# Hybrid SSD / RG-LRU block: output projections as seven half-block products, FFN pairs with running sums in PSUM

## The chip, the cores and the metric

The kernel runs on one core of one Trainium2 chip. The metric is the device time of one execution in microseconds, as the median of three runs. A profile is one more execution, recorded by the hardware profiler; its times are measured from the first instruction of its span. The engines are TensorE (PE in the profile, with its weight loads as PEld), VectorE (DVE), ScalarE (ACT), GpSimd (POOL) and SyncE (SP), which issues all the data transfers of this kernel.

## The reference, cut to what matters

One layer, 1024 tokens, width 1024, float32. The change concerns the two output projections, the merge of their results, and the gate/up products of the FFN:

```python
hn = rmsnorm(h, norm1_w)
proj = hn @ w_in                                   # gates, z, xBC, dt, lru_x, lru_y
y_ssm = mamba2_mixer(...) @ w_out_ssm              # 2048 -> 1024
y_lru = rglru_mixer(...) @ w_out_lru               # 1280 -> 1024
h = h + (g_ssm * y_ssm + g_lru * y_lru) @ w_out    # 1024 -> 1024
hn = rmsnorm(h, norm2_w)
gate, up = split(hn @ w_ffn_in, 2)                 # 1024 -> 2 x 2816
h = h + (silu(gate) * up) @ w_ffn_out              # 2816 -> 1024
return rmsnorm(h, norm_f_w)
```

## The kernel before

Activations lie transposed: features on the 128 partitions, tokens along the row, in two token halves of 512 (`hcol`). A float32 product is made of three matmuls with operands rounded to fp32r: every operand is split into a high part (a cast on ScalarE, L99) and the rest (a subtraction on VectorE, L100), and `mm3` (L168 to 177) or `product` (L947 to 954) issues hi·hi, lo·hi and hi·lo for each 128-row block of the contraction, 128x128 weights against 128x512 activations, into one PSUM bank. All instructions are laid in order by a scheduler at compile time: on each engine the earliest instruction of the program that is ready by its own reckoning comes next, and a tile takes whichever buffer of its pool is free. The chip then runs each engine's list strictly in order.

The stages that matter here, in order of time:

1. **Input projection, with the SSD and then the LRU mixer beside it.** The last part loops over ten LRU blocks `j`: two projections of 48 matmuls and `lru_gates(j)` (L780 to 815). Mixer outputs go to DRAM as 128x1024 tiles, `yn_d[0..15]` (SSD) and `yl_d[0..9]` (LRU). Before the last two gate projections the kernel already loads and splits the first half of `yn_d[0..7]` (`y0`, L831).
2. **SSD output projection** (L868 to 884): the 2048 rows in two halves `q`; for each `q`, each of 8 output column tiles `d` and both token halves a product of 8 blocks, 24 matmuls. At `q` = 0 the bank is copied into `res[d]` by ScalarE (L879), at `q` = 1 it is added by VectorE (L881) and the sum is scaled by the gate (L883).
3. **LRU output projection** (L887 to 900): for each `d` and half one product of 10 blocks, 30 matmuls; VectorE scales it by its gate (L895) and adds it to `res` (L896), and the merged `mg` is split into operands.
4. **w_o stage** (from L973): 16 products of 24 matmuls, the residual added from `xT`, squares summed on POOL (L864), and in its second half the differences `t1` to `t4` for the FFN made on VectorE by `t_parts` (L956 to 967).
5. **FFN pairs**: the gate and up tiles of one hidden block `n` are taken as a 2x2 block product with seven half-block products instead of eight (12 matmuls each, `product`); `first_pair` (L1017) and then 21 times `pair` (L1051). POOL makes the weight sums (`pair_sums`, L924 to 933). Partial results stand in several banks (`px`, `pv`, `py`, `pz`) and are put together on VectorE in `c0` and `c1`.
6. **FFN output** (L1090 to 1207): rows 0 to 2047 in two parts of eight blocks; each part is a seven-product scheme over four pairs of column tiles (`d` and `d + 4`). A part has 14 slots (seven products `N2, N5, N3, N1, N6, N7, N4`, each for two groups `g` of two column pairs), and each slot has 24 matmuls. Loads, weight sums (`w_sum`, POOL, L1158 and L1161), operand splits (`x_part`, `w_part`) and products are hung on slots: `w_part` of a product one slot ahead, its `x_part` two. The operands `act_d` and their differences `t_d` come from DRAM; the differences are made by `t_store` on VectorE while the pairs run. After each product VectorE adds the bank to `res` (L1206).
7. The last 6 hidden blocks by plain products, the final norm and the stores.

Pools that the steps touch: `wpool` holds `raw`, `whi`, `wlo` with two buffers each; `ar` 22 units, `ar0` 8, `br` 6 and `wq` 5 units of 128x1024; `pb` the 8 PSUM banks; `sp1` 5 and `tp` 10 tiles of 128x512.

Of the kernel before, what the change touches and what calls it, by code (L numbers as in the profile page):

```python
# [8 lines left out]
F32 = mybir.dt.float32  # L9
# [6 lines left out]
P = 128  # L16
# [44 lines left out]
NTMP = 10  # L61
# [7 lines left out]
def hybrid_block(ctx, tc, xT, w_in, w_dt, w_os, w_ol, w_o, w_fi, w_fo, w_fl, lru_w, params, heads, out):  # L69
# [66 lines left out]
    wseq += [(w_os[d, q], 8) for q in range(2) for d in range(KD)]  # L136
    wseq += [(w_ol[d, :, 5 * q : 5 * q + 5], 5) for d in range(KD) for q in range(2)]
# [6 lines left out]
    wstop = [wseq_out]  # L144
# [137 lines left out]
    res_d = [dram.tile([P, T], F32, name=f"res_d{i}") for i in range(KD)]  # L282
    t_d = [dram.tile([P, T], F32, name=f"t_d{i}") for i in range(8 * NPART)]
    act_d = [dram.tile([P, T], F32, name=f"act_d{i}") for i in range(NFF)]

# [3 lines left out]
    with ExitStack() as st1:  # L289
# [474 lines left out]
        with tc.tile_pool(name="lru", bufs=1, reuse_waits="tile", side="right") as lp, tc.tile_pool(  # L764
# [51 lines left out]

            for j in range(NLRU):
                project_now(lx_done(j))
                project_now(lg_done(j))
                lru_gates(j)  # L820

# [30 lines left out]
    def load_acts(pool, srcs, h):  # L852
        return [act_pair(pool, load_half(s[:, hcol[h]])) for s in srcs]

    def mm_act(ps, w, xs):
        mm3(ps, lambda k: (w[0][:, k, :], w[1][:, k, :]), xs)

    def sumsq(acc, src, first):
        if first:
            S.activation(acc, src, AF.Square)  # L860
        else:
            sq = temp("sq2")
            S.activation(sq, src, AF.Square)  # L863
            G.tensor_tensor(acc, acc, sq, op=ALU.add)  # L864


    res = [unit(br if d < 6 else ar, F32, "res") for d in range(KD)]
    for q in range(2):  # L868
        yn = [
            y0 if q == 0 and h == 0 else load_acts(ar0 if h == 0 else ar, yn_d[q * 8 : q * 8 + 8], h) for h in range(2)  # L870
        ]
        for d in range(KD):
            w = next_w()
            for h in range(2):
                ps = bank()
                mm_act(ps, w, yn[h])
                r = res[d][:, h, :]
                if q == 0:
                    S.copy(r, ps)  # L879
                else:  # L880
                    V.tensor_tensor(r, r, ps, op=ALU.add)  # L881
                    gt = load_half(gate_d[d][:, hcol[h]], "gt")
                    V.scalar_tensor_tensor(r, gt, 1.0, r, op0=ALU.add, op1=ALU.mult)  # L883


    yl = [load_acts(ar, yl_d, h) for h in range(2)]
    mg = [[None] * KD for _ in range(2)]  # L887
    for d in range(KD):
        w = next_w(), next_w()
        for h in range(2):  # L890
            ps = bank()
            mm3(ps, lambda k: (w[k // 5][0][:, k % 5, :], w[k // 5][1][:, k % 5, :]), yl[h])
            r = res[d][:, h, :]
            gt = load_half(gate_d[8 + d][:, hcol[h]], "gt")
            V.scalar_tensor_tensor(gt, gt, 1.0, ps, op0=ALU.add, op1=ALU.mult)  # L895
            V.tensor_tensor(r, r, gt, op=ALU.add)  # L896
        mg[0][d] = act_pair(ar0, res[d][:, 0, :])
    for d in range(KD):
        mg[1][d] = act_pair(ar, res[d][:, 1, :])
# [9 lines left out]
    row = lambda t_: t_.rearrange("p a b -> p (a b)")  # L909
# [15 lines left out]
    def pair_sums(n):  # L925
# [5 lines left out]
        G.tensor_tensor(u_[:, 0:4, :], u_[:, 0:4, :], g_[:, 0:4, :], op=ALU.add)  # L931
        G.tensor_tensor(g_[:, 0:4, :], g_[:, 0:4, :], blk(s1), op=ALU.add)
        G.tensor_tensor(g_[:, 4:8, :], g_[:, 4:8, :], g_[:, 0:4, :], op=ALU.add)
# [13 lines left out]
    def product(ps, w, xs, first, last):  # L947
        n = len(xs)
        for k in range(n):
            wh, wl = w[0][:, k, :], w[1][:, k, :]  # L950
            xh, xl = xs[k]
            PE.matmul(ps, wh, xh, start=first and k == 0, stop=False, skip_group_check=True)  # L952
            PE.matmul(ps, wl, xh, start=False, stop=False, skip_group_check=True)  # L953
            PE.matmul(ps, wh, xl, start=False, stop=last and k == n - 1, skip_group_check=True)  # L954

    def t_parts(x, k, u1, u2, pool):  # L956


# [10 lines left out]

# [4 lines left out]
    for h in range(2):  # L974
        for i, d in enumerate(wo_order[h]):
# [14 lines left out]
            if h == 0:  # L990
                bn[d] = unit(br if d not in (0, 4) else ar, F32, "bn")
# [58 lines left out]
    def pair(n, nxt, pump):  # L1050
# [36 lines left out]
        finish_pair(n, c0, c1)  # L1087

# [311 lines left out]
```

## Time and profile before

| | us |
|---|---|
| median of three runs | 2101.86 (2101.03 to 2103.66) |
| the profiled execution | 2103.04 |
| its span, first to last instruction | 2101.2 |
| PE busy | 2056.3 (98%) |
| DVE busy | 1300.4 (62%) |
| ACT busy | 868.8 (41%) |
| POOL busy | 448.2 (21%) |

Matmuls overlap, so that PE's busy time says little about single matmuls: one is recorded with some 390 ns, while in an undisturbed stretch one starts every 227 ns. What a stage costs is therefore read from the length of its window and its count of matmuls; waits of PE and its granted clock show where it fell behind.

### The profile page before, as it was taken

How to read it: one execution, taken by the hardware profiler on the slowest of the kernel's cores; microseconds unless marked ns; L12 is line 12 of the kernel's file. 1: busy time of each engine (PE TensorE's matmuls, PEld its weight loads, DVE VectorE, ACT ScalarE, POOL GpSimd, SP SyncE). 2: the span in 40 equal slices, each digit the busy share in tenths (PEclk: the TensorE clock that was granted, in tenths of full speed). 3: DMA queues.
4: the chain of work that ended last, by engine and by line, in shares of the span. 5: the costliest groups of instructions: out<-in, count | busy, mean ns of one | idle time of the engine just before them, and what ended most of it. 6: DMA issues, size and time to landing. Idle time of an engine off the chain costs nothing.

```text
span 2101.2 us, 24820 instructions
## 1 busy us (share of the span) xinstructions
PE 2056.3 (98%) x9650; PEld 1669.8 (79%) x9650; DVE 1300.4 (62%) x1582; ACT 868.8 (41%) x1227; POOL 448.2 (21%) x390
## 2 busy tenths in 40 slices
PE   8999999999999999999999999998999999989998
PEld 6677887887887888888878888876887888877888
DVE  8655567568667546655513543578577577588745
ACT  5334445445445436666523221453222222234334
POOL 5103333234333410000000000123322332342200
PEclk8999999999999999999999999999999999999999
DMA  3222223323223242221334532452244254286122
GB/s 141 89 60 87 89 76 118 100 67 120 93 76 115 89 145 81 69 77 65 105 115 146 153 120 63 149 177 77 79 173 154 75 180 161 86 290 209 61 59 87
DMA packets 106500, 235.22 MB, mean 112 GB/s; under 512 B 11920, under 2 KB 30352, under 8 KB 106384
## 3 DMA queue, kind: packets, MB, share of 16 engines
q1 hardware_dynamic: 106384, 233.66, 33.6%
q8 instruction: 75, 1.23, 0.2%
q14 instruction: 41, 0.34, 0.1%
HBM read 183.02 MB, written 50.59 MB: 111 GB/s over the span
## 4 chain that ended last, share of the span: by engine, by line
PE 83%; DVE 7%; DMA 3%; ACT 3%; issue 2%; POOL 1%; SPq 1%; DVEq 0%; ACTq 0%
PE pj L177 11%; PE pj L175 11%; PE pj L176 11%; PE pbk L952 8%; PE pbk L953 8%; PE pbk L954 8%; PE pbk L175 7%; PE pbk L177 7%; PE pbk L176 7%; PE yb L662 1%; DVE wlo L100 1%; PE yb L650 1%; DVE xs L495 1%; PE tr L628 1%; DMA ld<-yn_d 1%
## 5 line engine op out<-in xcount | busy, mean ns | idle before, releaser
L175 PE MATMUL pj<-hnh,whi 128*128 128x512 f32 x1152 | 461.1, 400 | 0.0
L177 PE MATMUL pj<-hnl,whi 128*128 128x512 f32 x1152 | 452.9, 393 | 0.0
L176 PE MATMUL pj<-hnh,wlo 128*128 128x512 f32 x1152 | 452.4, 393 | 0.0
L100 DVE TENSOR_TENSOR wlo<-raw,whi 128x1024 fp32r<-128x1024 f32 (+2 forms) x156 | 193.4, 1240 | 139.1 <-ACT whi L99 138.1
L177 PEld LDWEIGHTS pj<-hnl,whi 128*128 128x128 f32 x1152 | 216.6, 188 | 48.1 <-issue 0.5
L175 PEld LDWEIGHTS pj<-hnh,whi 128*128 128x128 f32 x1152 | 216.8, 188 | 46.1 <-issue 2.4
L176 PEld LDWEIGHTS pj<-hnh,wlo 128*128 128x128 f32 x1152 | 217.0, 188 | 45.0 <-issue 1.4
L99 ACT CAST whi<-raw 128x1024 fp32r<-128x1024 f32 (+2 forms) x156 | 156.1, 1001 | 212.2 <-PE pbk L177 103.0
L175 PE MATMUL pbk<-un,whi 128*128 128x512 f32 x544 | 212.3, 390 | 0.4 <-ACT un L99 0.3
L177 PE MATMUL pbk<-un,whi 128*128 128x512 f32 x544 | 212.1, 390 | 0.0
L176 PE MATMUL pbk<-un,wlo 128*128 128x512 f32 x544 | 211.8, 389 | 0.3 <-DVE wlo L100 0.3
L864 POOL TENSOR_TENSOR rs<-rs,sq 128x512 f32<-128x512 f32 x14 | 24.1, 1723 | 637.7 <-ACT sq L863 637.7
L621 ACT ACTIVATE E<-csb,cs 128x128 f32<-128x128 f32 x256 | 82.8, 392 | 108.2 <-PE yb L662 101.2
L177 PEld LDWEIGHTS pbk<-un,whi 128*128 128x128 f32 x544 | 102.1, 188 | 22.7 <-DVE un L100 1.6
L175 PEld LDWEIGHTS pbk<-un,whi 128*128 128x128 f32 x544 | 102.1, 188 | 22.3 <-ACT un L99 1.2
L176 PEld LDWEIGHTS pbk<-un,wlo 128*128 128x128 f32 x544 | 102.1, 188 | 22.1 <-DVE wlo L100 0.7
L99 ACT CAST wsh<-raw 128x1024 fp32r<-128x1024 f32 x44 | 46.1, 1050 | 165.7 <-PE pbk L954 147.4
L954 PE MATMUL pbk<-xtl,wsh 128*128 128x512 f32 x264 | 104.5, 396 | 0.0
L953 PE MATMUL pbk<-xth,wsl 128*128 128x512 f32 x264 | 104.3, 395 | 0.0
L952 PE MATMUL pbk<-xth,wsh 128*128 128x512 f32 x264 | 103.7, 405 | 0.0
L953 PE MATMUL pbk<-xph,wlo 128*128 128x512 f32 x224 | 88.1, 394 | 7.2 <-DVE wlo L100 7.2
L930 POOL TENSOR_TENSOR ws<-raw 128x512 f32<-128x512 f32 x22 | 31.1, 1412 | 282.7 <-DMA raw<-in_w_fi 241.7
(295 smaller groups left out, 4007.0 us busy)
## 6 DMA issues: line engine op xcount, KB each, us to landing
raw<-in_w_in SPq DMA_DIRECT2D x74, 512.0 KB, 3.5
raw<-in_w_fi SPq DMA_DIRECT2D x44, 512.0 KB, 3.5
csb<-cs_d SPq DMA_DIRECT2D x64, 256.0 KB, 3.5
act_d<-c SPq DMA_DIRECT2D x22, 512.0 KB, 2.6
yn_d<-xs SPq DMA_DIRECT2D x16, 512.0 KB, 3.3
ld<-yn_d SPq DMA_DIRECT2D x32, 256.0 KB, 4.8
raw<-in_w_os SPq DMA_DIRECT2D x16, 512.0 KB, 3.5
gt<-gate_d SPq DMA_DIRECT2D x32, 256.0 KB, 4.3
```

The costliest lines, as they stand in the source:

```text
L99: S.copy(hi, src)
L100: V.tensor_tensor(lo, src, hi.bitcast(F32), op=ALU.subtract)
L175: PE.matmul(ps, wh, xh, start=i == 0, stop=False)
L176: PE.matmul(ps, wl, xh, start=False, stop=False)
L177: PE.matmul(ps, wh, xl, start=False, stop=i == n - 1)
L495: V.scalar_tensor_tensor(dst[:, s:], ps[:, : T - s], taps[3 - s], dst[:, s:], op0=ALU.mult, op1=ALU.add)
L621: S.activation(E[:, j, :], csb[:, j, :], AF.Relu, bias=cs[:, c, h0 + j : h0 + j + 1], scale=-1.0)
L864: G.tensor_tensor(acc, acc, sq, op=ALU.add)
L930: G.tensor_tensor(blk(s1), u_[:, 0:4, :], u_[:, 4:8, :], op=ALU.add)
L952: PE.matmul(ps, wh, xh, start=first and k == 0, stop=False, skip_group_check=True)
L953: PE.matmul(ps, wl, xh, start=False, stop=False, skip_group_check=True)
L954: PE.matmul(ps, wh, xl, start=False, stop=last and k == n - 1, skip_group_check=True)
```

## The change

- The SSD projection becomes two of the seven-product schemes that the FFN output already uses, one for each eight blocks of rows; the LRU projection becomes one scheme for its first eight blocks and a direct product for blocks 8 and 9. The scheme moves into a function `seven`, which all five uses share, and the products themselves become events of their slots.
- The differences that the schemes need (`ty_d`, `tl_d`) are made by `t_store` during the ten LRU blocks and go through DRAM; twelve calls in all. `y0` goes, and the weights of the two projections leave the prefetched sequence.
- The first terms of an output block are copied from the bank by ScalarE in the first SSD scheme, later ones are added by VectorE. Gates are loaded as 128x1024 tiles into `wq`; SSD gates are applied in `gate_res`, LRU gates and the merge in `merge`, hung on the products `N6`, `N7` and `N4` of the LRU scheme.
- The FFN pairs change signs and order, so that four products run into one bank `pu` that is read in between; ScalarE copies three banks, and VectorE's subtractions fall away.
- The w_o stage takes its temporaries from `sp1` in place of `tp`, and `wq` is opened earlier.

```diff
@@ weights @@
-    wseq += [(w_os[d, q], 8) for q in range(2) for d in range(KD)]
-    wseq += [(w_ol[d, :, 5 * q : 5 * q + 5], 5) for d in range(KD) for q in range(2)]
+    wseq_in = len(wseq)
...
-    wstop = [wseq_out]
+    wstop = [wseq_in]
@@ LRU blocks @@
+    def t_store(pool, src, dst, k, swap=False):
+        u1, u2 = unit(pool, F32, "tu"), unit(pool, F32, "tu")
...
+        V.tensor_tensor(u1[:, 0], u1[:, 1], u1[:, 0], op=ALU.subtract)
+        V.tensor_tensor(u1[:, 1], u2[:, 1], u1[:, 1], op=ALU.subtract)
+        yield
+        V.tensor_tensor(u2[:, 1], u2[:, 1], u1[:, 0], op=ALU.subtract)
+        V.tensor_tensor(u2[:, 0], u2[:, 0], u2[:, 1], op=ALU.subtract)
+        store(dst[k], row(u1))
+        store(dst[k + 4], row(u2))
...
             for j in range(NLRU):
+                ts = [t_store(ar0, yn_d, ty_d, tys[j])] if j < 8 else []
+                if j >= 6:
+                    ts.append(t_store(ar0, yl_d, tl_d, j - 6, True))
+                for t_ in ts:
+                    next(t_)
                 project_now(lx_done(j))
                 project_now(lg_done(j))
                 lru_gates(j)
+                for t_ in ts:
+                    for _ in t_:
+                        pass
@@ the scheme @@
+    def seven(c0_, act, tdf, w_of, out, pools=None, xpool=None, swap=False, done=None):
...
+        def products(n, g):
...
+                product(banks[p], (hi[:, a], lo[:, a]), xop[n], first, last)
+                d = q * 4 + p
+                r, new = out(d, 1 - h if swap else h)
+                if new and n in (N2, N5, N3, N4):
+                    S.copy(r, banks[p])
+                else:
+                    V.tensor_tensor(r, r, banks[p], op=ALU.add)
+                if done:
+                    done(n, d)
+
+        for g in range(2):
+            at(c0_ - 4 + g, load_w, 0, 1, g)
+            at(c0_ - 3 + g, load_w, 1, 0, g)
+            at(c0_ - 3 + g, load_w, 1, 1, g)
+            at(c0_ - 2 + g, load_w, 0, 0, g)
+            for n in range(7):
+                at(c0_ + 2 * n - 4 + g, load_xop, n, g)
+                at(c0_ + 2 * n - 2 + g, x_part, n, g)
+                at(c0_ + 2 * n + g - 1, w_part, n, g)
+                at(c0_ + 2 * n + g, products, n, g)
+            at(c0_ + g, w_sum, 1, g)
+            at(c0_ + 1 + g, w_sum, 2, g)
+            at(c0_ + 2 + g, w_sum, 4, g)
+            at(c0_ + 5 + g, w_sum, 3, g)
...
+    def gate_res(d):
+        gt = load_gate(d)
+        V.scalar_tensor_tensor(row(res[d]), row(gt), 1.0, row(res[d]), op0=ALU.add, op1=ALU.mult)
...
+    def merge(d, h=None):
+        if d not in gl_t:
+            gl_t[d] = load_gate(8 + d)
+        v = row if h is None else (lambda t_: t_[:, h, :])
+        r, y = v(res[d]), v(yo[d])
+        V.scalar_tensor_tensor(y, v(gl_t[d]), 1.0, y, op0=ALU.add, op1=ALU.mult)
+        V.tensor_tensor(r, r, y, op=ALU.add)
+        for i in range(2):
+            if h in (None, i):
+                mg[i][d] = act_pair(ar, res[d][:, i, :])
...
+    def merged(n, d):
+        if n == N6:
+            merge(d)
+        elif n == N7:
+            merge(d, 0)
+        elif n == N4:
+            merge(d, 1)
...
+    DIR = 2 * CYC
+    for i in range(2):
+        seven(i * CYC, yn_d[8 * i : 8 * i + 8], ty_d[8 * i : 8 * i + 8], ..., out_res(i),
+              xpool=ar0 if i == 0 else None)
+    seven(DIR + 4, yl_d[:8], tl_d, ..., lambda d, h: (yo[d][:, h, :], False), swap=True, done=merged)
...
+        at(DIR - 2 + i, direct_load, i)
+        at(DIR - 2 + i, direct_x, i)
+        at(DIR + 2 * i, direct, i)
+    for d in range(KD):
+        at(DIR + d, gate_res, d)
@@ pair @@
-        px, pv = bank(), bank()
-        product(px, wo["a11"], x["b11"], True, False)
-        S.copy(c1[:, 0, :], px)
+        pu, pv, px = bank(), bank(), bank()
+        product(pu, wo["a11"], x["b11"], True, False)
+        S.copy(c0[:, 0, :], pu)
         product(pv, wo["s1"], x["t1"], True, False)
-        product(px, wo["a12"], x["b21"], False, True)
+        S.copy(c1[:, 1, :], pv)
+        product(pu, wo["s2"], x["t2"], False, False)
+        S.copy(c0[:, 1, :], pu)
...
+        product(px, wo["a12"], x["b21"], True, True)
+        V.tensor_tensor(c0[:, 0, :], c0[:, 0, :], px, op=ALU.add)
...
+        product(pu, wo["s3"], x["t3"], False, False)
+        V.tensor_tensor(c1[:, 1, :], c1[:, 1, :], pu, op=ALU.add)
...
         product(pv, wo["s4"], x["b22"], False, True)
         V.tensor_tensor(c0[:, 1, :], c0[:, 1, :], pv, op=ALU.add)
+        product(pu, wo["a22"], x["t4"], False, True)
+        V.tensor_tensor(c1[:, 0, :], pu, rs2[0], op=ALU.mult)
...
```

`first_pair` changes in the same way: `a11` goes into `pu`, `a12` into a bank of its own, and the copy of `pu` (`S.copy(c0[:, 0, :], pu)`) stands after the third product.

## Rows read from the trace of the kernel before

**Rows 1.** The page: span, part 1 (busy us, share), part 5 (one group).

```profile
span 2101.2 us, 24820 instructions
...
PE 2056.3 (98%) x9650; PEld 1669.8 (79%) x9650; DVE 1300.4 (62%) x1582; ACT 868.8 (41%) x1227; POOL 448.2 (21%) x390
...
L175 PE MATMUL pbk<-un,whi 128*128 128x512 f32 x544 | 212.3, 390 | 0.4 <-ACT un L99 0.3
```

**Rows 2.** Windows by stage: LRU, SSD out, LRU out, w_o, first pair, pairs, FFN out twice.

```profile
core 0: us, PE busy (x) PEld busy (x) DVE busy (x) ACT busy (x) POOL busy (x), PEclk, DMA share, GB/s
780.00:1043.60 263.60, 263.29 (x1151) 215.90 (x1151) 152.13 (x129) 167.01 (x161) 0.00 (x0) 1.00 0.24 81
1043.60:1217.60 174.00, 173.57 (x760) 142.00 (x759) 63.68 (x85) 48.81 (x73) 0.00 (x0) 1.00 0.42 138
1217.60:1326.60 109.00, 109.00 (x483) 90.21 (x482) 46.99 (x69) 23.90 (x36) 0.00 (x0) 1.00 0.30 92
1326.60:1417.10 90.50, 90.22 (x396) 74.05 (x395) 58.51 (x59) 47.99 (x65) 21.88 (x13) 1.00 0.55 177
1417.10:1448.40 31.30, 23.20 (x88) 17.73 (x87) 29.77 (x27) 12.63 (x16) 15.04 (x10) 0.84 0.13 44
1448.40:1858.10 409.70, 409.62 (x1765) 329.47 (x1764) 270.16 (x309) 111.11 (x127) 115.47 (x81) 1.00 0.40 138
1858.10:1944.60 86.50, 79.26 (x337) 63.91 (x336) 77.50 (x66) 35.67 (x37) 34.00 (x12) 0.98 0.66 231
1944.60:2020.80 76.20, 76.20 (x338) 63.12 (x337) 50.04 (x55) 24.39 (x27) 11.35 (x4) 1.00 0.15 49
```

**Rows 3.** PE's waits from 1040 to 2021 us: total, times, longest.

```profile
PE pbk L953 <- DVE wlo L100: 8.1, 5, 4.3
PE pbk L952 <- ACT c L1024: 7.2, 1, 7.2
```

**Rows 4.** Groups by shape, FFN output, 1858 to 2020 us: busy, mean ns, idle before.

```profile
L100 DVE TENSOR_TENSOR xpl<-xr,xph 128x1024 fp32r<-128x1024 f32 x26 | 43.7, 1684 | 4.7 <-ACT xph L99 2.8 <-PE pbk L953 1.6
...
L1206 DVE TENSOR_TENSOR res<-res,pbk 128x512 f32<-128x512 f32 x55 | 37.1, 681 | 21.2 <-PE pbk L954 21.2
...
L1158 POOL TENSOR_TENSOR raw<-raw,ws 128x1024 f32<-128x1024 f32 x4 | 13.0, 3255 | 0.3
```

**Rows 5.** Timeline, 1870 to 1878 us: start, us, engine and line, idle before it.

```profile
1871.29 1.21 DVE L100 TENSOR_TENSOR xpl<-xr,xph 128x1024 fp32r<-128x1024 f32 x1
...
1871.44 3.31 POOL L1158 TENSOR_TENSOR ws<-ws,wr 128x1024 f32<-128x1024 f32 x1 [3.49 <-DVE wlo L100]
...
1872.42 3.41 DVE L100 TENSOR_TENSOR wlo<-ws,whi 128x1024 fp32r<-128x1024 f32 x1
```

**Rows 6.** Groups by shape on DVE in the LRU blocks, 780 to 1043.6 us.

```profile
L812 DVE SCALAR_TENSOR_TENSOR u<-u,lth 128x1024 f32<-128x1024 f32 x10 | 12.3, 1225 | 11.0 <-ACT lth L810 11.0
...
L814 DVE TENSOR_TENSOR a<-a,gl 128x1024 f32<-128x1024 f32 x10 | 12.1, 1215 | 0.0
```

**Rows 7.** Groups by shape in the two projections, 1100 to 1330 us.

```profile
L100 DVE TENSOR_TENSOR un<-ld,un 128x512 fp32r<-128x512 f32 x36 | 23.6, 690 | 9.2 <-ACT un L99 9.2
```

**Rows 8.** Timeline, 1423 to 1434 us, at the first FFN pair.

```profile
1425.67 1.05 ACT L99 CAST xth<-bn 128x1024 fp32r<-128x1024 f32 x1 [7.77 <-DVE bn L960]
...
1427.77 0.56 ACT L1024 COPY c<-pbk 128x512 f32<-128x512 f32 x1
...
1428.38 0.80 PE L952 MATMUL pbk<-un,whi 128*128 128x512 f32 x1 [7.21 <-ACT c L1024]
...
1428.98 0.63 PE L953 MATMUL pbk<-un,wlo 128*128 128x512 f32 x1
...
1432.64 1.22 DVE L100 TENSOR_TENSOR wsl<-raw,wsh 128x1024 fp32r<-128x1024 f32 x1
```

**Rows 9.** Groups by shape in the 21 pairs, 1448.4 to 1858.1 us.

```profile
L1071 DVE TENSOR_TENSOR c<-c,pbk 128x512 f32<-128x512 f32 x21 | 14.4, 687 | 31.4 <-PE pbk L954 31.4
...
L1060 ACT COPY c<-pbk 128x512 f32<-128x512 f32 x21 | 11.9, 569 | 3.2 <-PE pbk L954 3.2
```

More of the change, by code (lines that the diff above doesn't have):

```diff
@@ L60 @@
 WARM = 12
-NTMP = 10
 NUNIT = 22
@@ L861, in sumsq @@
         else:
-            sq = temp("sq2")
+            sq = temp2("sq2")
             S.activation(sq, src, AF.Square)
             G.tensor_tensor(acc, acc, sq, op=ALU.add)
[L867 to L873, printed above, removed]
+    blk = lambda t_: t_.rearrange("p (k c) -> p k c", c=P)
@@ new lines, in product @@
+    def product(ps, w, xs, first, last):
+        n = len(xs)
+        for k in range(n):
+            wh, wl = w[0][:, k, :], w[1][:, k, :]
+            xh, xl = xs[k]
+            PE.matmul(ps, wh, xh, start=first and k == 0, stop=False, skip_group_check=True)
+            PE.matmul(ps, wl, xh, start=False, stop=False, skip_group_check=True)
+            PE.matmul(ps, wh, xl, start=False, stop=last and k == n - 1, skip_group_check=True)
+    N2, N5, N3, N1, N6, N7, N4 = range(7)
+    CYC = 14
@@ new lines, in hybrid_block, with direct_load, direct_x @@
+    yo = []
+    dw, dx = [], []
+    def direct_load(i):
+        t_ = wpool.tile([P, KD, P], F32, name="raw", tag="raw", bufs=2)
+        for a in range(4):
+            load(t_[:, 2 * a : 2 * a + 2], w_ol[i * 4 + a, :, 8:10])
+        hi, lo = (wpool.tile([P, KD, P], F32R, name=x, tag=x) for x in ("whi", "wlo"))
+        split(hi, lo, t_)
+        dw.append((hi, lo))
+    def direct_x(i):
+        u = unit(ar0, F32, "dx")
+        load(row(u), yl_d[8 + i])
+        hi, lo = unit(ar0, name="dxh"), unit(ar0, name="dxl")
+        split(row(hi), row(lo), row(u))
+        dx.append((hi, lo))
@@ L874, in hybrid_block, with direct @@
+    def direct(i):
+        for a in range(4):
+            yo.append(unit(ar0, F32, "yo"))
             for h in range(2):
                 ps = bank()
[L876 to L883, printed above, removed]
@@ L898, in hybrid_block @@
-    for d in range(KD):
-        mg[1][d] = act_pair(ar, res[d][:, 1, :])
-    blk = lambda t_: t_.rearrange("p (k c) -> p k c", c=P)
-    row = lambda t_: t_.rearrange("p a b -> p (a b)")
+                w = dw[i]
+                product(
+                    ps,
+                    (w[0][:, 2 * a : 2 * a + 2], w[1][:, 2 * a : 2 * a + 2]),
+                    [(x[0][:, h], x[1][:, h]) for x in dx],
+                    True,
+                    True,
+                )
+                S.copy(yo[-1][:, h, :], ps)
@@ L910, in hybrid_block @@
+    later |= {direct, gate_res}
+    for i in range(2):
+        at(DIR - 2 + i, direct_load, i)
+        at(DIR - 2 + i, direct_x, i)
+        at(DIR + 2 * i, direct, i)
+    for d in range(KD):
+        at(DIR + d, gate_res, d)
+    for s in sorted(events):
+        run(s)
+    events.clear()
     raws, wops = {}, {}
@@ L1127, in load_res @@
         load(row(res[d]), res_d[d])
-    def load_w(i, q, kh, g):
-        if (q, kh) == (0, 1):
-            t_ = wpool.tile([P, KD, P], F32, name="raw", tag="raw", bufs=2)
-            t_ = t_.rearrange("p (a k) c -> p a k c", a=2)
-        else:
-            t_ = unit(ar if i == 0 and q == 1 else ar0, F32, "wr").rearrange("p a (k c) -> p a k c", c=P)
-        for a in range(2):
-            load(t_[:, a], w_fo[q * 4 + 2 * g + a, :, i * 8 + kh * 4 : i * 8 + kh * 4 + 4])
-        wr[i, q, kh, g] = t_
@@ L1190, in hybrid_block @@
     for d in range(KD):
         at(-1 + d // 4, load_res, d)
[L1192 to L1206 removed]
+        events[-1 + d // 4].insert(0, events[-1 + d // 4].pop())
@@ L1268, in w_last @@
         return wts
-    def temp2(name):
-        return sp1.tile([P, H], F32, name=name, tag="ws1")
     def finish(t0, t1, acc, sq):
```

302 lines of the change are left out of this document (145 added, 157 removed).

## The prediction

> **What bounds the kernel now.** I read the page first: PE is busy for 98% of the span [rows 1], so matmuls taken away shorten the kernel if the other engines keep up. Then the windows by stage, for what a matmul costs and where PE fell behind. The SSD projection takes 174.0 us for 768 matmuls (2 halves x 8 tiles x 2 token halves x 24), which is 226.6 ns for one; the LRU projection 109.0 us for 480, the same [rows 2]. Neither loses anything worth naming. The FFN output runs the very scheme that the change brings into both projections: two parts of 336 matmuls. The second takes 76.2 us, 226.8 ns a matmul; the first 86.5 us, 10.3 us more, at 77.5 us of DVE work and 34.0 us of POOL, against 50.0 and 11.4 in the second [rows 2]. PE's waits name what was late there: the low part of the weights from VectorE, 8.1 us in five waits. The other large one is 7.2 us at a ScalarE copy in `first_pair` [rows 3].
>
> **Part 1: matmuls.** One scheme has 14 slots x 24 = 336 matmuls in place of 384, and two cover SSD: 672 for 768. The 544 of each kind on the page [rows 1] are 256 of SSD, 160 of LRU and 128 of `w_o`. LRU: 336, and the direct blocks 8 tiles x 2 halves x 2 blocks x 3 = 96, together 432 for 480. That is 144 fewer, and 144 x 226.6 ns = **-32.6 us**, all of it on PE's path. The FFN keeps its 84 matmuls for a pair.
>
> **Part 2: the start of the SSD scheme.** Its first operands come from `ar0`, its weights through `raw`, both free before the last two gate projections end. I have no such start in the trace; the nearest are the two FFN schemes: +10.3 us where the last pair's work lay beside it, 0 where it did not. Between them I take +3, nearer to 0, since VectorE has 152 us of work in 264 us of the LRU blocks [rows 2] and 16 of the first scheme's 28 banks are read by ScalarE. The second scheme has 28 splits (1.22 us) and 28 additions (0.68 us) [rows 4, 5], 53 us in 76; price 0, bounds 0 and 3.
>
> **Part 3: direct blocks and the start of the LRU scheme.** `yo[4..7]` need units of `ar0` that the direct operands hold until the last direct product, so all eight banks fill before ScalarE's first copy; PE then waits for one copy, 0.57 us [rows 9], and for a split queued behind eight of them. `gate_res` adds 8 x 1.23 us to VectorE. I take +2, bounds 0 and 10.3.
>
> **Part 4: the merge, the largest cost.** In the slots of N6, N7 and N4 VectorE gets: four whole merges (1.23 + 1.22 for the gate and the sum, two splits of 0.69, so 3.82 each [rows 6, 7]) = 15.3 us; eight half merges of three instructions of 0.69 = 16.6; nine operand splits of 1.22 = 11.0; twelve additions of 0.68 = 8.2. Together 51.1 us in 61 instructions. Back to back each starts some 0.08 us before the one ahead is recorded as ended (1871.29 + 1.21 against 1872.42 [rows 5]), so 46 us. PE needs 6 x 24 x 0.2266 = 32.6. A merge stands ahead of the next slot's `w_part` in the program, and VectorE takes the earliest ready instruction, so the merges delay the low parts of the weights, and at the end those of the first `w_o` weights. If all of it is late, PE loses 46 - 32.6 = 13.4 us; by the recorded durations 18.5; if the splits slip through ahead of the merges, nearly nothing, because `mg` of the second half is needed only 43 us later. I take **+13**, bounds 0 and 18: where VectorE had more to do than PE before (the first pair, 29.8 us in 31.3), PE did wait. Each merge also waits for its gate. Two of `wq`'s five units hold `res`, so three gates are in flight, and the gate of the last tile can be loaded only after the first merge of N4; the `w_o` weights may stand behind that load on SP's queue. I leave that inside the 13.
>
> **Part 5: what moves into the LRU blocks.** Twelve `t_store` calls, 4 half subtractions each: 48 x 0.69 = 33 us for VectorE, less 8 splits of `y0` (5.5). It has 111 us free there, POOL does nothing in that window [rows 2], and the loads are issued an iteration ahead. Price 0, bounds 0 and 3; if that cover failed PE would see the 2.8 us of a call per block.
>
> **Part 6: the first pair.** The 7.2 us wait is for a copy that stood on ScalarE behind a cast which itself waited 7.8 us for VectorE [rows 8]. With `a12` in a bank of its own PE no longer waits there. But what is late next is on the same chain: the products after `a12` need `wsl`, which VectorE finished at 1432.64 + 1.22 = 1433.9, and `a12` had just ended then [rows 8]. The wait moves, it does not go. I take -1, bounds -10 (the wait and the half-speed clock behind it gone: a matmul is recorded with 0.63 in place of 0.39 us, and the window's clock is 0.84 [rows 2, 8]) and +3 (temporaries from five `sp1` tiles).
>
> **Part 7: the pairs.** A pair takes 409.7 / 21 = 19.51 us, and 84 x 0.2266 = 19.03. No wait of a bank is in the list, for instance none at L1071 [rows 3, 9]: the scheduler already lays other matmuls between a bank's reading and its next use. VectorE loses two instructions a pair, 1.4 us, ScalarE gets two more of 0.57 [rows 9]; neither bounds. -1 for the stage, bounds -10 (all the excess) and +5. The FFN output keeps its schedule, with the residuals loaded first at its start: 0, bounds -3 and 3.
>
> **Sum**, against the profiled execution's 2103.0: -32.6 + 3 + 0 + 2 + 13 + 0 - 1 - 1 = -16.6, so 2086.4. That execution lies 1.2 us over the median of 2101.86, so I predict **2085**.
>
> **A rule against the change.** Beside a POOL sum of 3.31 us a split of VectorE took 3.41 us instead of 1.21, and ended 1.08 us after the sum [rows 5]. [...] What it does here, from rows: 53 us of VectorE work in a scheme and 8 sums of about 3.2 us [rows 4] make 79 us, more than the 76.2 that PE needs. That is the third rival.
>
> **Rivals.**
> - *The splits go first.* The merges fall back into the slack of the `w_o` stage (VectorE 58.5 us in 90.5 [rows 2]); of the 13 us some 2 remain: 2085 - 11 = 2074. For it: nothing but the order holds a split back. Against: program order.
> - *The first pair's wait goes.* If the schedule finds other products ready (`s1` with its first two blocks), 9 us more are won: 2076.
> - *POOL's sums starve every scheme*; the case on the other side. Each of the three schemes pays what the first FFN one did, 10.3 us, in place of my 3 + 0 + 2, and the merges come on top: 2085 + 31 - 5 = 2111. It decides the sign from about 7 us a scheme. For it: 77.5 us of VectorE in that window. Against: the second FFN scheme paid nothing.
> - *The running sums make a wait*, so that part of the change does the opposite of what it says. `pu` is read after `s2` and written again one product later, 2.7 us. ScalarE needs 0.57 and may have two casts and a `silu` of 1.05 us ahead: 3.7 us, 1 us over. At 0.6 us in each of 21 pairs: +13, 2098.
>
> **How the numbers follow.** Forecast 0.45 (2077 to 2097 by its own bounds), splits first 0.25, first pair 0.10, sums starve 0.12, running sums 0.08. The range runs from 2066, the first rival with free starts and some of the first pair, to 2106, between forecast and starved schemes; about 0.1 lies above it and less below. A measurement of this kernel can tell about 0.2%, 4.2 us, from no change: faster is below 2097.7. The forecast, but for a few hundredths, and the first two rivals make 0.78; the running sums and the forecast's upper edge 0.10 for the same; the starved schemes 0.12 for slower.
>
> **What would show it.** In the changed kernel's windows the two SSD schemes should take 76 to 80 us each, the direct blocks and LRU scheme 100 to 115, with PE's waits at the low parts of `whi`/`wlo` in N7, N4 and the first `w_o` product, and VectorE without a pause there. If that window has no waits, part 4 is wrong. If schemes take over 83 us with POOL busy, parts 2 and 3 are. The first pair should still hold 7 us or more of waiting, now at `wsl` or `xtl`. Pairs should take 19.4 to 19.5 us; 20 or more would show waits for `pu`.

## The result and the profile after

The changed kernel takes 2174.45 us (median, 2173.65 to 2175.62) against 2102.76 of the kernel before beside it: 1.034 times as long, 95% interval 1.0322 to 1.0358. I had forecast 2085 and a range up to 2106. Its profiled execution has these parts of the page (span, busy time by engine, and the group of matmuls with the largest wait: busy, mean ns | idle before, by what):

```profile
span 2173.9 us, 24882 instructions
PE 2061.8 (95%) x9506; PEld 1664.6 (77%) x9506; DVE 1401.4 (64%) x1626; ACT 934.4 (43%) x1291; POOL 516.4 (24%) x414
L905 PE MATMUL pbk<-xth,wsh 128*128 128x512 f32 x264 | 115.2, 436 | 45.4 <-ACT c L1265 44.8
```

PE has 144 matmuls less and is busy longer: 95% of a longer span in place of 98% [rows 1]. The windows say where. The stages are the LRU blocks, first and second SSD scheme, direct blocks, LRU scheme, `w_o`, first pair, 21 pairs, and the two FFN output schemes; they answer to [rows 2].

```profile
core 0: us, PE busy (x) PEld busy (x) DVE busy (x) ACT busy (x) POOL busy (x), PEclk, DMA share, GB/s
780.00:1043.30 263.30, 262.78 (x1149) 215.22 (x1149) 180.21 (x172) 165.95 (x156) 0.00 (x0) 1.00 0.49 174
1043.30:1135.70 92.40, 79.79 (x337) 64.49 (x336) 57.10 (x43) 41.48 (x48) 33.08 (x11) 0.93 0.61 208
1135.70:1211.90 76.20, 76.20 (x338) 63.06 (x336) 64.75 (x59) 29.16 (x29) 24.43 (x9) 1.00 0.54 181
1211.90:1234.80 22.90, 22.00 (x97) 17.79 (x96) 11.60 (x9) 7.72 (x13) 3.38 (x2) 1.00 0.52 175
1234.80:1318.80 84.00, 79.20 (x337) 63.81 (x337) 68.40 (x78) 31.83 (x40) 11.34 (x4) 0.98 0.25 78
1318.80:1415.30 96.50, 91.71 (x388) 74.38 (x386) 63.93 (x69) 50.32 (x69) 21.54 (x13) 0.96 0.54 167
1415.30:1446.30 31.00, 23.76 (x88) 16.87 (x87) 30.42 (x26) 13.46 (x18) 16.87 (x10) 0.94 0.16 52
1446.30:1926.70 480.40, 435.60 (x1765) 346.88 (x1764) 246.91 (x265) 135.81 (x169) 112.06 (x81) 0.95 0.34 118
1926.70:2017.40 90.70, 82.23 (x337) 65.62 (x336) 76.97 (x67) 36.61 (x38) 31.91 (x11) 0.92 0.64 223
2017.40:2093.60 76.20, 76.20 (x338) 63.07 (x337) 49.93 (x55) 24.39 (x27) 11.36 (x4) 1.00 0.16 48
```

Two things stand out. The pairs take 480.4 us in place of 409.7: +70.7, the whole loss. And both projections together take 92.4 + 76.2 + 22.9 + 84.0 = 275.5 us. With the first `w_o` matmul as the boundary, as here, they took 285.0 before and `w_o` 88.5 (in [rows 2] the boundary lies 2 us earlier): -9.5 and not -32.6, with `w_o` 8.0 and the first FFN output scheme 4.2 longer. The half that should have paid nets about zero. PE's waits over all these stages (total, times, longest):

```profile
PE pbk L905 <- ACT c L1265: 44.8, 19, 3.5
PE pbk L905 <- ACT whi L98: 10.2, 2, 9.3
PE pbk L906 <- DVE wlo L99: 7.8, 6, 3.0
PE pbk L907 <- DVE xpl L99: 6.3, 4, 3.6
PE pbk L174 <- DVE wlo L99: 3.8, 2, 3.6
```

L1265 is ScalarE's copy of `pu` after the product `s2` in `pair`; PE waits for it in 19 of 21 pairs. L98 and L99 are the cast and the subtraction of a split (L99 and L100 before), L905 to L907 the matmuls of `product`. One pair shows what the copy waits for. ScalarE, POOL and PE, each by start and duration, with the idle time before an instruction and its releaser:

```profile
1520.82 0.62 ACT L98 CAST ws1h<-ws 128x512 fp32r<-128x512 f32 x1 [1.24 <-POOL ws L1145]
1525.26 1.04 ACT L98 CAST wsh<-raw 128x1024 fp32r<-128x1024 f32 x1 [3.81 <-POOL raw L1148]
1526.21 0.58 ACT L1265 COPY c<-pbk 128x512 f32<-128x512 f32 x1
```

```profile
1519.50 1.29 POOL L1145 TENSOR_TENSOR ws<-raw 128x512 f32<-128x512 f32 x1 [17.81 <-DMA raw<-in_w_fi]
...
1523.94 1.28 POOL L1148 TENSOR_TENSOR raw<-raw 128x512 f32<-128x512 f32 x1
```

```profile
1521.37 0.39 PE L907 MATMUL pbk<-xtl,wsh 128*128 128x512 f32 x1
...
1524.12 0.39 PE L907 MATMUL pbk<-un,whi 128*128 128x512 f32 x1
1526.84 0.50 PE L905 MATMUL pbk<-xth,wsh 128*128 128x512 f32 x1 [2.33 <-ACT c L1265]
...
1528.35 0.63 PE L905 MATMUL pbk<-xth,wsh 128*128 128x512 f32 x1
1528.77 0.63 PE L906 MATMUL pbk<-xth,wsl 128*128 128x512 f32 x1
```

The last matmul of `s2` started at 1521.37 (the first PE row), and the copy was ready soon after. But ScalarE's list has the cast `wsh` of the *next* pair's weights ahead of it, and that cast waits 3.81 us for the last of POOL's four weight sums. In the program the copy stands before this cast; it is the compile-time schedule, by its own reckoning of what is ready, that put them the other way round, and the chip kept to that list. So the copy runs at 1526.21, and `s3`, which adds to `pu`, starts at 1526.84, after the 12 matmuls of `a12` that the schedule had put between. Two edits of the change meet here. It added two copies to ScalarE's list in every pair, of which this one has a product waiting right behind it. And it exchanged the order of the two casts: `pair_s` now takes `q` = 0 (`s2`, `s4`) first, which needs all four sums, where before `q` = 1 came first, released by the second sum (L931) after a wait of 0.76 us. In the kernel before:

```profile
1515.15 1.05 ACT L99 CAST wsh<-raw 128x1024 fp32r<-128x1024 f32 x1 [0.76 <-POOL raw L931]
```

No run takes back the exchange alone, so what each of the two edits adds is not shown.

### The profile page after: what moved, and what is told of

It reads as the page before. It is cut to its first block, busy times and chain, and to the rows that moved or that the text cites. A ratio compares the mean times of both kernels' runs of the same rounds, so it can differ in the third digit from the quotient of the medians.

```text
span 2173.9 us, 24882 instructions
## 1 busy us (share of the span) xinstructions
PE 2061.8 (95%) x9506; PEld 1664.6 (77%) x9506; DVE 1401.4 (64%) x1626; ACT 934.4 (43%) x1291; POOL 516.4 (24%) x414
## 3 DMA queue, kind: packets, MB, share of 16 engines
q8 instruction: 74, 1.21, 0.2%
## 5 line engine op out<-in xcount | busy, mean ns | idle before, releaser
L905 PE MATMUL pbk<-xph,whi 128*128 128x512 f32 x560 | 221.1, 396 | 13.4 <-ACT whi L98 10.2
L906 PE MATMUL pbk<-xph,wlo 128*128 128x512 f32 x560 | 221.8, 396 | 6.0 <-DVE wlo L99 6.0
L907 PE MATMUL pbk<-xpl,whi 128*128 128x512 f32 x560 | 220.4, 396 | 6.4 <-DVE xpl L99 6.3
L99 DVE TENSOR_TENSOR wlo<-raw,whi 128x1024 fp32r<-128x1024 f32 (+1 forms) x138 | 181.2, 1314 | 52.4 <-ACT whi L98 52.3
L98 ACT CAST whi<-raw 128x1024 fp32r<-128x1024 f32 (+1 forms) x138 | 142.5, 1033 | 96.6 <-PE pbk L175 32.0
L905 PE MATMUL pbk<-xth,wsh 128*128 128x512 f32 x264 | 115.2, 436 | 45.4 <-ACT c L1265 44.8
L98 ACT CAST wsh<-raw 128x1024 fp32r<-128x1024 f32 x44 | 45.9, 1048 | 226.0 <-issue 137.0
L905 PEld LDWEIGHTS pbk<-xph,whi 128*128 128x128 f32 x560 | 107.0, 191 | 37.7 <-ACT whi L98 11.0
L907 PEld LDWEIGHTS pbk<-xpl,whi 128*128 128x128 f32 x560 | 107.2, 191 | 31.3 <-DVE xpl L99 9.2
L906 PEld LDWEIGHTS pbk<-xph,wlo 128*128 128x128 f32 x560 | 106.9, 191 | 30.5 <-DVE wlo L99 7.9
L99 DVE TENSOR_TENSOR xpl<-xr,xph 128x1024 fp32r<-128x1024 f32 x70 | 113.4, 1626 | 24.1 <-ACT xph L98 19.2
L98 ACT CAST xph<-xr 128x1024 fp32r<-128x1024 f32 x70 | 72.7, 1049 | 97.4 <-DVE xpl L99 53.5
L907 PE MATMUL pbk<-xtl,wsh 128*128 128x512 f32 x264 | 113.4, 430 | 0.6 <-DVE xtl L99 0.6
```

The costliest lines, as they stand in the source:

```text
L98: S.copy(hi, src)
L99: V.tensor_tensor(lo, src, hi.bitcast(F32), op=ALU.subtract)
```

## The experiments

### The pairs

Two runs split the change in its halves, two more test why the pairs are slow. e1 is the changed kernel with the pairs of before:

```diff
-    finish_pair, first_pair, pair, pair_sums, t_parts of after
+    finish_pair, first_pair, pair, pair_sums, t_parts of before
```

> The changed kernel with the FFN pairs, their weight sums and differences as they were before; the projections stay changed. In the changed kernel the 21 pairs take 480.2 us (23.3 each on the mean of 20) against 409.5 before. If all of the loss lies in the pairs and nothing is coupled, 2174.5 - 70.7 = 2104, the pairs at 19.5 us each and the projections at 275.5 us as in the changed kernel. If the new pools (wq opened earlier, operands in other pools) slow the pairs whatever their code is, it stays above 2130.

Measured: 2102.94 us beside 2102.19 of before, ratio 1.0005 (0.9996 to 1.0015). The projections alone are worth nothing, and they lose nothing.

e2 is the reverse, the kernel before with the changed pairs.

```diff
-    finish_pair, first_pair, pair, pair_sums, t_parts of before
+    finish_pair, first_pair, pair, pair_sums, t_parts of after
```

> The kernel before with the changed pairs alone. If the pairs' own code is the cause: 2102.8 + 70.7 = 2173, pairs at 23.3 us, PE waiting for the copy of the running sum. If the loss needs the new pools too: about 2103.

Measured: 2173.98 us, ratio 1.0342 (1.0327 to 1.0358). PE's largest wait is the same there (L1060 is the copy's line in that kernel):

```profile
PE pbk L952 <- ACT c L1060: 44.3, 19, 2.8
```

So the loss is the pairs', by themselves. e3 keeps all products, banks and copies and changes only the order on ScalarE's list: the copy is pinned ahead of the cast (`pin` lets each pinned instruction of an engine follow the one pinned before it).

```diff
-        split(row(hi), row(lo), raws[n][q]...)
+        cast = S.copy(row(hi), src)
+        if q == 0 and n > 1:
+            pin(cast)
+        V.tensor_tensor(row(lo), src, row(hi)..., op=ALU.subtract)
...
-        S.copy(c0[:, 1, :], pu)
+        pin(S.copy(c0[:, 1, :], pu))
```

> The changed kernel; on ScalarE the copy of the running sum after s2 is ordered ahead of the cast of the next pair's first weight sums, nothing else: same copies, same banks. Theory A, ScalarE's order (the copy stands behind a cast that waits for POOL's last weight sum): the wait goes, pairs 19.5 us, total 2104. Theory B, ScalarE has too many copies: unchanged, 2174. Theory C, one bank read and written again one product later is too tight: unchanged, 2174.

Measured: 2104.3 us, ratio 1.0008 (0.9998 to 1.0017), and the pairs' window

```profile
1444.50:1855.10 410.60, 408.84 (x1766) 331.12 (x1765) 245.64 (x265) 136.21 (x169) 112.38 (x81) 1.00 0.39 138
```

at full clock. On ScalarE's timeline the copy (now L1269) runs 0.29 us after it became idle, and the cast, now at L1159 and the last row here, still waits for POOL's last sum:

```profile
1530.70 0.59 ACT L1269 COPY c<-pbk 128x512 f32<-128x512 f32 x1 [0.29 <-PE pbk L907]
1534.24 1.05 ACT L1159 CAST wsh<-raw 128x1024 fp32r<-128x1024 f32 x1 [2.95 <-POOL raw L1148]
```

The cause is shown: neither the number of copies nor the shared bank costs anything here, only the place of one copy in one list. e4 moves the copy to another engine instead:

```diff
-        S.copy(c0[:, 1, :], pu)
+        V.tensor_copy(c0[:, 1, :], pu)
```

> The changed kernel; the copy of the running sum after s2 made by VectorE instead of ScalarE. Theory A (order on ScalarE): the wait goes, 2104, if VectorE's own list does not put the copy behind something that waits; theory B (too many copies on ScalarE): two copies are left for one before, so 2104 to 2140; theory C (bank too tight): unchanged, 2174.

Measured: 2104.62 us, ratio 1.0012 (1.0003 to 1.0021). Either cure gives back the 70 us; against before, both versions of the pairs stand within 1 us in 410.

### Where the 32.6 us of the projections went

All further runs build on e3. Its stages, against 336 matmuls at 226.6 ns = 76.1 us for a scheme, lose 16 us at the start of the first SSD scheme, 8 in the LRU scheme and 6.6 in `w_o` (95.1 for 88.5). For the start, one theory was that too few matmuls lie ahead of the first product that needs POOL's sums. e5 puts the product N1, which needs no sum, second, gives each running group its own bank and shifts the second and third sum by two slots:

```diff
-            for n in range(7):
+            for p_, n in enumerate((N2, N1, N5, N3, N6, N7, N4) if c0_ == 0 else range(7)):
...
-                    banks[p] = bank()
+                    banks[key] = bank()
```

> On top of e3: in the first scheme of the SSD projection and in the first of the FFN output the product N1, whose operands need no weight sum, runs ahead of N5 and N3, and the sums that follow N5 move two slots later. In e3 the first SSD scheme takes 92.5 us against 76.2 for the second, the first of the FFN output 90.8. Theory A, the chain from the late weight loads over POOL's sums to the splits has too few slots of cover: N1 covers 10.9 us more, so the first schemes fall to 77 to 81 us, total 2104 - 23 = 2081. Theory B, VectorE is starved by POOL for the whole scheme, whatever the order: 90 us or more each, total 2104.

Measured: 2108.78 us, ratio 1.0033 (1.002 to 1.0045). The first SSD scheme takes 91.6 us in place of 92.5, and the first FFN output scheme 94.7 in place of 90.8: a second product that needs no sum cures neither start.

e6 takes the merges out of the LRU scheme's last slots: halves with index 0 follow at slots 10 to 13, the other halves are merged one tile at a time in the first half of `w_o`.

```diff
     def merged(n, d):
-        if n == N6:
-            merge(d)
-        elif n == N7:
-            merge(d, 0)
-        elif n == N4:
-            merge(d, 1)
+        if n == N6 or n == N7:
+            at(DIR + 4 + 10 + d // 2, merge, d, 0)
...
             w = next_w()
+            if h == 0:
+                merge(d, 1)
```

> On top of e3: the merges of the LRU scheme are made by halves; the half that the w_o stage needs first is hung two slots after its product, behind the operand splits of that slot, the other half is merged one tile at a time in the first half of the w_o stage. Same work on VectorE (less 8 instructions that took whole tiles and more that take halves), gates loaded by halves into sp1. In e3 the LRU scheme takes 84.2 us and the w_o stage 95.2, against 76.2 without waits and 88.5 before. Theory A (merges stand ahead of the splits): 77 and 89 to 91, total 2104 - 12 = 2092. Theory B (the waits are for something else, such as the gates' loads or the ar units): unchanged, 2104.

Measured: 2090.03 us (2087.38 to 2096.75), ratio 0.9953 (0.994 to 0.9967). The LRU scheme and `w_o`, first of e3, then of e6:

```profile
1234.20:1318.40 84.20, 79.40 (x338) 63.84 (x337) 68.52 (x78) 31.80 (x40) 11.34 (x4) 0.98 0.23 78
1318.40:1413.50 95.10, 90.16 (x387) 73.35 (x386) 64.25 (x69) 50.16 (x69) 21.71 (x13) 0.98 0.51 170
```

```profile
1233.60:1309.90 76.30, 76.30 (x338) 63.14 (x338) 63.42 (x75) 30.44 (x37) 11.35 (x4) 1.00 0.25 85
1309.90:1399.00 89.10, 88.50 (x388) 72.26 (x386) 72.54 (x80) 52.09 (x72) 20.59 (x13) 1.00 0.57 191
```

13.9 us come back, 7.9 and 6.0, though VectorE has no less work: 5.1 us of it leave the first window and 8.3 us come into the second. In the changed kernel the end of the merge is plain on VectorE's timeline: five instructions of merge, and only then the low part of the first `w_o` weights, for which PE has waited 3.56 us. e6 also loads the gates in another way, but from 1315.67 us up to this split VectorE has no pause: it is held by its own order and not by a load.

```profile
1319.88 1.33 DVE L1077 SCALAR_TENSOR_TENSOR yo<-gt,yo 128x512 f32<-128x512 f32 x2
1321.13 1.29 DVE L1078 TENSOR_TENSOR res<-res,yo 128x512 f32<-128x512 f32 x2
1322.34 0.68 DVE L1077 SCALAR_TENSOR_TENSOR yo<-gt,yo 128x512 f32<-128x512 f32 x1
1322.94 1.22 DVE L99 TENSOR_TENSOR wlo<-raw,whi 128x1024 fp32r<-128x1024 f32 x1
```

```profile
1324.21 0.80 PE L174 MATMUL pbk<-un,wlo 128*128 128x512 f32 x1 [3.56 <-DVE wlo L99]
```

e7 has the edits of e5 and e6 together, and no others.

> e5 and e6 together with e3's order on ScalarE. If the three losses are separate: 2104 - 23 - 12 = 2069, 33 us under the kernel before, which is what the 144 matmuls are worth. If the time won in one stage is lost in the next (VectorE's backlog): 2080 to 2090.

Measured: 2093.81 us, ratio 0.9966 (0.9955 to 0.9978): nothing over e6. e8 tests another suspect, the first FFN output scheme, in which the change loads the residuals first; here, on e3, they come behind the scheme's own loads again.

```diff
-        events[-1 + d // 4].insert(0, events[-1 + d // 4].pop())
+        (the event is put behind the last load_w, load_xop or load_res of its slot)
```

> On top of e3: at the start of the FFN output the residuals are again loaded behind the operands and weights of their slot, as in the kernel before. The first FFN scheme took 86.5 us before and 90.8 in e3. If the order of the loads is the cause: 86.5 again, total 2104 - 4 = 2100. If it is the products' place among the events (additions ahead of splits): unchanged, 2104.

Measured: 2107.86 us, ratio 1.0032 (1.0019 to 1.0044); that scheme takes 92.3 us, not less. The order of these loads is not its cause.

### The start of the first SSD scheme

In the changed kernel PE has 48 matmuls to do and then stands still. Two windows (PE alone; in the second the granted clock is 0.62 on the mean and the DMA engines are full), the loads on SP's queue, and POOL's first sum:

```profile
1043.30:1054.30 11.00, 11.00 (x49) 1.00 0.84 277
1054.30:1066.30 12.00, 1.24 (x3) 0.62 1.00 363
```

```profile
1044.66 0.32 SPq L80 DMA_DIRECT2D gate_d<-gl  x1
1045.02 5.46 SPq L77 DMA_DIRECT2D wr<-in_w_os  x10
1051.41 2.46 SPq L77 DMA_DIRECT2D xr<-ty_d  x2
```

```profile
1053.78 2.48 POOL L962 TENSOR_TENSOR ws<-wr 128x1024 f32<-128x1024 f32 x1 [299.33 <-DMA wr<-in_w_os]
```

This sum has ended at 1056.26, but its cast runs only 6.3 us later: on ScalarE's list it stands behind two casts of the differences `ty_d`, which wait for their loads.

```profile
1058.97 1.04 ACT L98 CAST xph<-xr 128x1024 fp32r<-128x1024 f32 x1 [4.03 <-DMA xr<-ty_d]
1061.60 1.04 ACT L98 CAST xph<-xr 128x1024 fp32r<-128x1024 f32 x1 [1.58 <-DMA xr<-ty_d]
1062.55 1.04 ACT L98 CAST whi<-ws 128x1024 fp32r<-128x1024 f32 x1
```

PE's wait of 9.3 us ends with this cast, at 1063.64. The product needs the first of those differences as well, so by these rows the order on ScalarE cost at most 1063.64 - (1058.97 + 1.04) = 3.6 us of it, an estimate; the rest is the wait for the loads.

The weights' loads are issued right behind the last store of the input projection, at its end, because `ar`, into which they go, is opened over memory of the LRU blocks. e9, on e6, gives three of `ar`'s units to `ar0`, which is there earlier, and loads the first group's weights into them.

```diff
-NUNIT = 22
+NUNIT = 19
...
-        ar0 = ctx.enter_context(tc.tile_pool(name="ar0", bufs=8, ...))
+        ar0 = ctx.enter_context(tc.tile_pool(name="ar0", bufs=11, ...))
...
-                t_ = unit(pools.get((q, kh), ar), ...)
+                t_ = unit(pools.get((q, kh, g), pools.get((q, kh), ar)), ...)
...
+            pools={"s1": ar, **({k: ar0 for k in ((1, 0, 0), (1, 1, 0), (0, 0, 0))} if i == 0 else {})},
...
-                x2["b22"][k] = act_pair(ar, b)
+                x2["b22"][k] = act_pair(ar0 if k < 3 else ar, b)
```

> On top of the merges that come later (2090, first SSD scheme 92.5 us): three units of ar become units of ar0, and the first group's three weight tiles of the first SSD scheme are loaded into them, so that they are issued ahead of the last gate store and not behind it. Theory A, the first scheme starves because its weights and differences are loaded only when the input projection has ended (12 loads of 256 KB issued from 1043.8 us, first weight sum at 1051.8): the sum can begin some 8 us sooner and the loads of ty_d stand 4 places further forward; first scheme 82 to 86 us, in all 2080 to 2084. Theory B, the chain behind the loads (weight sums on POOL, splits on VectorE that wait for one another) takes the time by itself: at most 3 us, 2087 to 2090.

Measured: 2089.26 us, ratio 0.9937 (0.9925 to 0.995). The scheme takes 87.8 us, 4.7 less: between the two theories; the whole is less than 1 us under e6, in the range of Theory B. The first of the first group's sums now runs at 1025.01 us, but the differences `ty_d` come late still, and the cast of that sum runs at 1059.00, again behind the casts that wait for them. e10 also has the sums `s1` of both SSD schemes in `wq`:

```diff
-            pools={"s1": ar, **(...)},
+            pools={"s1": wq, **(...)},
```

> As the run before, and the weight sums s1 of both SSD schemes stand in wq in place of ar. Theory A: the same start, 82 to 86 us for the first scheme, and the second group's loads find units a little sooner; 2078 to 2084. Theory B: 2087 to 2090.

Measured: 2087.12 us, ratio 0.9924 (0.9911 to 0.9938), the scheme 86.2 us: by the total Theory B again. The cast of the first sum runs at 1047.07, ahead of the casts of `ty_d`. With PE's wait for the weights gone, VectorE's timeline shows what is late next: four splits of 128x1024, 13.39 us, while POOL runs sum after sum (second group, one row of it):

```profile
1058.22 13.39 DVE L99 TENSOR_TENSOR xpl<-xr,xph 128x1024 fp32r<-128x1024 f32 x4
```

```profile
1060.46 3.37 POOL L959 TENSOR_TENSOR wr<-wr 128x1024 f32<-128x1024 f32 x1
```

That is 3.35 us a split, and the last of the four ends 1.08 us after the last of the four sums beside them (1070.53). The traces of both kernels show the same. In the kernel before, from 1858 to 1945 us, eight splits of 128x1024 started while a POOL sum ran: each ended 1.08 to 1.09 us after that sum and took 1.74 to 3.43 us, where the 22 that met no sum took 1.21 to 1.23. In the first SSD scheme of the changed kernel seven started so; they ended 1.08 to 1.09 us after their sums and took 2.01 to 3.42 us. The next two expectations call this the exclusion. e11 has the eight sums of this scheme on VectorE in place of POOL:

```diff
+            E = V if c0_ == 0 and act[0] is not act_d[0] else G
-            sub = lambda o, a, b: G.tensor_tensor(o, a, b, op=ALU.subtract)
+            sub = lambda o, a, b: E.tensor_tensor(o, a, b, op=ALU.subtract)
```

> On top of the run with early weights and early sums (2087, first SSD scheme 86.2 us): the eight weight sums of the first SSD scheme run on VectorE in place of POOL. Theory A, what is left of the start is the exclusion of VectorE's splits and POOL's sums (four splits took 13.4 us there in place of 4.9): the splits take 1.2 us again, eight sums cost VectorE some 10 us but none of it is blocked; first scheme 77 to 81 us, in all 2078 to 2083. Theory B, what is left is the loads of ty_d and yn_d behind the input projection: first scheme stays at 85 to 88 us, 2086 to 2090.

Measured: 2079.17 us, ratio 0.9894 (0.9878 to 0.9911); the scheme 82.7 us. The total lies in the range of Theory A, the scheme between the two. Of the 8.0 us won over e10 the scheme gives 3.5; another 2.9 lie in the first FFN output scheme (95.2 to 92.3), which was not edited. The splits of the differences and operands in that stage (1040 to 1120 us, by shape) have their own length again, and a sum on VectorE takes 1.2 us where POOL took up to 3.4:

```profile
L99 DVE TENSOR_TENSOR xpl<-xr,xph 128x1024 fp32r<-128x1024 f32 x15 | 18.4, 1232 | 5.5 <-PE pbk L906 3.1 <-DMA xr<-ty_d 1.2 <-ACT xph L98 1.0
```

So these splits take 1.21 to 1.39 us in this stage, and none is lengthened by POOL's sums as the four were in e10. But the edit also makes each sum shorter, so how much of the 3.5 us is the splits' and how much the sums' is not separated.

e12 does the same in the first FFN output scheme:

```diff
-            E = V if c0_ == 0 and act[0] is not act_d[0] else G
+            E = V if c0_ == 0 else G
```

> As the run before, and the eight sums of the first FFN output scheme on VectorE as well (95 us there in all runs with a shortened merge). Theory A, exclusion is what makes this scheme slow too: 95 falls to 80 to 86 us, 2064 to 2074 in all. Theory B, this scheme is late because its operands come late: within 3 us of the run before.

Measured: 2074.5 us (2071.94 to 2076.86), ratio 0.9869 (0.9854 to 0.9883): 1.3% under the kernel before, the best of all, and at the edge of Theory A. The two schemes of this run:

```profile
1041.40:1121.10 79.70, 76.85 (x338) 62.86 (x337) 52.44 (x49) 40.36 (x47) 10.40 (x4) 1.00 0.61 208
1829.70:1916.30 86.60, 81.24 (x338) 64.86 (x338) 76.11 (x76) 36.60 (x39) 11.33 (x4) 0.96 0.68 237
```

The FFN output scheme falls from 92.3 (e11) to 86.6 us, what it took before the change [rows 2]. Unedited, that scheme moved between 90 and 95 us in other runs, so this step is less sure than the one of e11. The first SSD scheme fell from 82.7 to 79.7 though nothing of it was edited: the compile-time schedule shifts with any edit, and steps of 3 us between two of these runs are not put down to a cause here.

## Why the prediction was wrong, point by point

The lengths of the stages in us (from one stage's first matmul to the next one's):

| stage | before | after | e3: copy first | e6: merges later | e12: weights early, sums on VectorE |
|---|---|---|---|---|---|
| SSD, LRU projections | 285.0 | 275.5 | 275.8 | 267.9 | 253.7 |
| w_o | 88.5 | 96.5 | 95.2 | 89.1 | 90.2 |
| first pair | 31.3 | 31.0 | 31.0 | 31.0 | 32.2 |
| 21 pairs | 409.7 | 480.4 | 410.6 | 410.0 | 412.1 |
| FFN output, first scheme | 86.5 | 90.7 | 90.8 | 95.1 | 86.6 |

- **Part 7, the pairs: the step that failed.** I took -1, bounds -10 to +5, because no bank had a wait before and two copies of 0.57 us are little work. Both are true and neither bears on it: what counts is what stands ahead of a copy on its in-order list, and what *that* waits for. The rival of the running sums named the right engine, bank and product. It counted the instructions ahead by their durations, "two casts and a `silu`", 1 us over the cover of 2.7; the chip had one cast ahead, with a wait of 3.81 us for POOL inside it. It came out at 13 us in 21 pairs. Measured: 44.8 us of waiting and 480.4 - 409.7 = 70.7 us in all. The difference, 435.6 - 409.6 = 26.0 us of PE's busy time for the same matmuls, is mostly the clock, which I had left out of the rival although I had priced it for the first pair: in the pair shown eight matmuls run at a pitch of 0.43 in place of 0.23 us, 1.6 us. After 15 of the 19 waits seven or eight do, after four none.
- **Part 1, the matmuls: right.** Where nothing waits, a scheme takes 76.2 us, 226.8 ns a matmul. e12 has the projections at 253.7 for 285.0, -31.3 of the -32.6.
- **Part 2, the start: mis-sized.** +3, bounds 0 to 10.3; measured 92.4 - 76.2 = +16.2. I looked at where the *first* operands go (`ar0`, `raw`: free early, and N2 did start at once) and not at where those of the second product go. Its weights go to `ar`, which opens with the end of the projection (e9: 4.7 us). Its differences are loaded behind those weights, and ScalarE casts its first weight sum only behind them: the same kind of list order as in part 7. The second scheme's price of 0 held: 76.2.
- **Part 3, direct blocks and the LRU start: right.** 22.9 us for 96 matmuls (21.8), so +1.1; the LRU scheme starts free, as e6 shows with 76.3.
- **Part 4, the merge: the mechanism right, the size in part luck.** +13, bounds 0 to 18; the stages that e6 shortens give 13.9. But my 13.4 was all waiting, and of the 13.9 PE's idle time is 9.1 (4.8 + 4.9 us before, 0.6 after); the other 4.8 are matmuls that ran slower, at a granted clock of 0.98 for both stages, which I had not priced. The place was right: low parts of the weights behind merges, up to the first `w_o` product. "Splits first", the rival at 2074, did not come by itself; e6 had to write it.
- **Part 5, `t_store`: right.** VectorE has 180.2 us in the LRU blocks in place of 152.1, +28.1 against the 27.5 forecast, and the window's length is the same.
- **Part 6, the first pair: right.** 31.0 for 31.3. The wait moved and split: 7.2 us of idle PE (31.0 - 23.8), 2.3 of it in one wait for `wsh`, the rest in smaller ones.
- **FFN output: +4.2**, over my bound of 3, and +8.6 in e6. With sums on VectorE it is 86.6 again (e12), but POOL made these sums in the kernel before too, so they alone do not explain what the change added. What moves it between 90 and 95 in the other runs stays open.
- **The third rival, POOL's sums starve every scheme:** half of it came. It did so in the first SSD scheme, once the loads were early (e10 to e11), and, less surely, in the first FFN scheme (e11 to e12); the second SSD scheme had 24.4 us of POOL beside 64.7 of VectorE and lost nothing. With POOL's sums gone the splits fall from 3.35 us (four in e10) to 1.23 (mean of 15 in e11). No run shows that every sum costs VectorE its whole length, as my 79 us had it: in the first SSD scheme of the changed kernel the seven splits that started during a sum took 21.0 us, 12.4 over 1.22 each, beside 33.1 us of POOL in all. Why a split waits for a sum is not shown.

With the pairs cured and nothing else (e3), the total of 2104 still lies 19 us over my 2085: 13 of them are part 2 and 4 the FFN output. In e12 two starts still lie over 76.2 us: the first SSD scheme by 3.5, the first FFN scheme by 10.4, as much as before the change.

## What to carry to other kernels

Before a PSUM bank is read in mid-group and written again, look at the reading engine's list and ask of each instruction ahead of the read what it waits for, not how long it runs: one cast that waits for POOL (3.81 us in the pair shown) cost 70 us in 21 pairs here, and moving it behind the copy cost nothing. Where a scheme starts at a stage's boundary, follow the buffers of its second product too, since memory that is opened at the boundary is loaded only from there. And sums on GpSimd were not free beside VectorE here: four splits took 3.35 us each beside them, and 15 took 1.23 on the mean with the sums on VectorE. Where a stage's start hung on both, VectorE alone was faster in both stages tried (86.2 to 82.7 us in e11, 92.3 to 86.6, less surely, in e12).

## What the runs showed of the hardware

- In the pair shown PE's granted clock fell from 1.00 to 0.50 *after* work had begun again: the wait of 2.33 us ends at 1526.84, six matmuls follow, most at 0.23 us, and then eight, from 1528.35 on, at 0.43 (granted clock 0.50 from 1528.4 to 1531.7). Of the 19 waits, 3 are followed by slow matmuls at once, 12 after up to 1.6 us of fast ones, and 4 by none: a wait of 2.28 us, which ends at 1550.33, leaves the clock at 1.00. Over the pairs' window the granted clock is 0.95, and 1.00 in e3. This wait of 2.3 us cost some 3.9 us; the mean of the 19 is 70.7 / 19 = 3.7. The windows behind these two waits:

```profile
1526.80:1534.00 7.20, 7.16 (x24) 0.76 0.00 0
1550.30:1557.50 7.20, 7.17 (x31) 1.00 0.55 207
```

- Four VectorE splits beside back-to-back POOL sums took 13.39 us, 3.35 each, where a split that met no sum took 1.21 to 1.23; moved to VectorE, each sum took 1.2 us there. Eight sums on VectorE made that stage shorter (86.2 to 82.7 us) although they are added to the engine that was late.
- Loads at the start of the SSD scheme ran at a DMA share of 1.00 with 363 GB/s, and there 12 loads of 256 KB and what follows them took longer than the 11 us that PE's first 48 matmuls cover.
